# Weights split once and kept in DRAM: the split parts of a two-layer trunk's weights are made in the first segment and loaded by the later ones

## The chip, the core and the metric

The kernel runs on one core of a Trainium2 chip, in one launch. The metric is device time in microseconds (us), from runs of the whole program. Three runs of the kernel before gave 3135.08, 3143.48 and 3137.76 us, with a median of 3137.76 us.

## What is computed

Two layers of a decoder trunk act on one sequence of 2048 tokens, 1024 features wide, in float32:

```
for l in range(DEPTH):                       # DEPTH = 2
    shift, scale, gate = split(silu(c) @ ada_w[l] + ada_b[l], 3)
    h = rms_norm(x, norm_g[l]) * (1 + scale) + shift
    y = even_mixer(h) if l == 0 else odd_mixer(h)
    x = x + gate * y
```

- Layer 0 (even): `h @ w_in` (1024 x 3072) feeds a gated linear recurrence (4 heads, key and value 128 wide) and a causal pooling mixer (windows 2, 4, 8, 16). Each is multiplied by a SiLU gate, and both are joined and multiplied by `w_out` (1024 x 1024).
- Layer 1 (odd): `h @ w_in` (1024 x 4112) gives q, k, v and a SiLU gate for 16 heads of 64, and a forget value per head. Attention is causal, with normalised q and k and the summed log-forget as a bias; then `w_out` (1024 x 1024).

## The kernel before

The 2048 tokens are cut into four segments of 512 (SEG). A segment goes through both layers before the next one begins, so every weight is used four times, once per segment. Matrix products run at float32 accuracy out of products of "fp32r" operands: each operand is kept as two parts, a rounded one and the rest (value minus rounded value), and each product is made of three passes (PASSES: first with first, first with second, second with first).

**Weights.** Each weight matrix is cut into tiles of 1024 x 256: 12 for layer 0's input projection (kind "a"), 4 for its output (kind "b"), 16 for layer 1's input (kind "c"), 4 for its output (kind "d"), 36 in all. The list `wseq` holds the order in which tiles are used, over all segments: 144 uses and one special last entry "e" (the last two blocks of layer 1's output weights, times the gate). A tile in SBUF, `wt`, holds both parts, 128 partitions x 16 KB = 2 MB, in two buffers.

`prep_w(n)` (line 272) makes the n-th tile. It has four pieces. Each piece is loaded by SP's DMA queue into `raw` (256 KB, four buffers); ACT casts it into the first part (`S.copy`, line 289), and DVE or POOL, by turns, subtracts to make the second (`split_lo`, line 178). For the very first tile POOL does all four. The casts and subtractions have a lowered priority (`tc.cur_priority += 80`). `next_w` (line 294) hands out tile n and calls `prep_w(n + 1)`, so the work for the next tile starts when the tile before this one has given its buffer back. The raw pieces themselves can be in SBUF earlier.

**Layer 0 of a segment** (`layer0`): four heads of the recurrence, woven with projections (`fill`), then `out_proj0` (line 830): tile b0, then b1, then b2 and b3 side by side, both held at once.

**Layer 1 of a segment** (`layer1`, line 1226): the rows are normed and turned, tile c0 gives the first q and k, then 16 heads of attention, four by four. In segment s, a head goes over 4(s+1) blocks of 128 keys (`attend`, line 1114). Per block PE makes two score products (`pst`), ACT makes the exponential twice (`p` in float32, line 1152; `ph` rounded, line 1154), DVE subtracts to get `pl` (line 178), POOL adds `p` to a running sum `la` (line 1162), and PE multiplies `ph` and `pl` with the values (`pov`), two blocks later (LAG = 2). Beside it `max_pass` (line 1083) makes the next head's maxima: PE makes `pmx`, DVE reduces it (line 1094). Keys and values of earlier segments come back from DRAM in chunks of four blocks: `K1o` (two buffers), `Vo` (two), and `K2o` (three buffers, shared by `attend` and `max_pass`). These loads run on SP's queue, as the weights do. The small rows `mr` (the maxima), `q4d` and `cfd` go over ACT's DMA queue. The next projections (tiles c1 to c15, then the next segment's a0 to a3, or in the last segment the d tiles) are woven in as `fill`.

The order of each engine's instructions is made by a scheduler that takes priorities and its own timing of the instructions; it is fixed before the run.

Of the kernel before, what the change touches and what calls it, by code (L numbers as in the profile page):

```python
# [8 lines left out]
F32 = mybir.dt.float32  # L9
F32R = mybir.dt.float32r  # L10
# [5 lines left out]
PSUM = bass.MemoryType.PSUM  # L16
DRAM = bass.MemoryType.DRAM

P = 128
T = 2048  # L20
D = 1024
ND = D // P          # blocks of the model's width
SEG = 512            # tokens that go through both layers together
NSEG = T // SEG
NTB = SEG // P       # token blocks of a segment
NH = 16              # heads of the attention
HD = 64
# [5 lines left out]
def trunk(ctx, tc, x, cvec, norm_g, ada_c, ada_w, ada_b, ada_bg, lbp, w0, w0o, w1, w1f, w1o,  # L33
# [57 lines left out]
    # mq[q, k]: keys after the query, in the last block; mk[k, q]: the same with keys on the partitions  # L91
# [16 lines left out]
    # ones between zeros: the columns from HD on fill a pair's first head, those from 0 on its second  # L108
# [5 lines left out]
    # masks of the halving levels: right halves of each block, compact, for the chunks of a segment  # L114
# [12 lines left out]
    # 1 / min(t + 1, w) for the first positions  # L127
# [28 lines left out]
    def rsqrt_mean(out_t, ss, n, name):  # L156
        """out = 1 / sqrt(ss / n + eps) on a small tile"""
# [12 lines left out]
    def silu_from(out_t, src, t):  # L170
        """out = src * sigmoid(src); src may lie in PSUM, t is scratch"""
        S.activation(t, src, AF.Exp, scale=-1.0)
        S.activation(t, t, AF.Ln, bias=1.0)
        S.activation(t, t, AF.Exp, scale=-1.0)
        V.tensor_tensor(out_t, src, t, op=ALU.mult)
# [5 lines left out]
    class Steps:  # L181
        """a queue of generators, taken a step at a time"""
# [27 lines left out]
    def weave(main, nm, fill, keep=0):  # L210
        """the main stream's steps with the fill's spread evenly among them, but for the last ones to keep"""
# [12 lines left out]
    def both(*l):  # L224
        """generators by turns, a step of each; a number bounds how many steps the one before it takes"""
# [39 lines left out]
    # the last two blocks of the last projection's four tiles, times the gate  # L265
# [3 lines left out]
    wready = {}  # L269
    wpos = [0]  # L270

    def prep_w(n):
        if n >= len(wseq) or n in wready:
            return
        late = wseq[n][0] == "e"
        src = None if late else wsrc[wseq[n][0]][wseq[n][1]]
        wt = wp.tile([P, 2, ND, 256], F32R, name="wt", tag="wt")
        parts = range(3 if late else 4)
        if not late and n >= len(wseq) - 5:
            parts = range((NEARLY[wseq[n][1]] + 1) // 2)  # L280
        for h in parts:
# [9 lines left out]
            tc.cur_priority -= 80  # L291
        wready[n] = wt
# [12 lines left out]
    def proj_T2(pts, wt, act):  # L305
        """two tiles of 128 features, the second half of the contraction for the first token blocks first"""
# [14 lines left out]
    def proj_T(pt, wt, fo, act):  # L321
        """pt[feature, token] = the weights' 128 columns from fo on; two steps"""
# [8 lines left out]
    def proj_N(pt, wt, act, tb, ds=tuple(range(ND)), first=True, last=True):  # L331
        """pt[token of block tb, 256 columns], all of the contraction or some blocks of it"""
# [14 lines left out]
    def mod_cols(l, b, pm, which, n):  # L347
        """n columns of the shift (which = 0) or the scale (1) from their sums"""
# [8 lines left out]
    # which engine sums a block of the shift's and scale's products over d: PE, Vector, GpSimd  # L357
    WHO = ("GV", "PV", "GV", "PV", "GV", "VV", "VV", "VV")

    def ada_first(half, slots, between):  # L360
        """shift and scale of half of layer 0's features"""
# [51 lines left out]
    def ada_rest(scratch):  # L413
        """layer 0's gate, layer 1's shift and scale: products on the vector engine, sums on PE"""
# [31 lines left out]
    def norm_rows(xr, xt, stat=None):  # L446
        """the rows over their root mean square"""
# [934 lines left out]
```

## Time and profile before

| | |
|---|---|
| median of three runs | 3137.76 us (3135.08 to 3143.48) |
| span of the profiled execution (the one time the profile gives for it) | 3139.8 us |
| PE (TensorE) busy | 2830.8 us, 90% |
| DVE (VectorE) busy | 2505.1 us, 80% |
| ACT (ScalarE) busy | 1780.4 us, 57% |
| POOL (GpSimd) busy | 1226.5 us, 39% |
| mean granted TensorE clock | 0.967 |
| moved by DMA | 337.99 MB, mean 108 GB/s |

Busy times are shares of the whole span; the profile can also be asked for stretches of it. A row of the groups by line names the line of the kernel, the engine, the operation, the tile written and the tiles read, the shape and how often it ran; then come the total time, the mean of one in ns, and the engine's idle time just before these instructions with what ended it.

### The profile page before, as it was taken

The page shows a single profiled execution, that of the slowest core. Times are in us where ns is not written, and L with a number is a line of the kernel's source. Part 1 is how long each engine was busy: PE and PEld are TensorE (multiplying, and loading weights), DVE is VectorE, ACT ScalarE, POOL GpSimd, SP SyncE. Part 2 cuts the span into 40 slices and gives each one's busy share as a digit, 9 for nine tenths or more (in the row PEclk, how much of TensorE's full clock was granted, in tenths as well). Part 3 has the DMA queues.
Part 4 walks back from the last instruction along what each step waited for, and adds up shares of the span by engine and source line. Part 5 has one row for each costly group of instructions (what it writes and reads, how often), then busy time and mean ns, then how long its engine had stood idle before and what let it go on. Part 6 is the DMA issues. An engine that isn't in the chain of part 4 may idle for free. (4 is left out here: it accounts for less than half of the span.)

```text
span 3139.8 us, 49278 instructions
## 1 busy us (share of the span) xinstructions
PE 2830.8 (90%) x17020; PEld 2393.2 (76%) x17020; DVE 2505.1 (80%) x4518; ACT 1780.4 (57%) x3679; POOL 1226.5 (39%) x944
## 2 busy tenths in 40 slices
PE   5999899999998888899998888889999988888888
PEld 4788788888787777789897767777988866666666
DVE  8776697875868787875768888898666889898997
ACT  3454566753555566663555665666344566666653
POOL 3221232232123444343214555555311265656564
PEclk9999999999999999999999999999999999999999
DMA  6423453333333333334234333332423322222232
GB/s 241 161 78 108 124 150 100 113 105 101 96 115 99 94 104 98 109 91 122 76 124 121 99 112 105 114 118 90 132 75 106 100 88 90 91 92 90 89 121 66
DMA packets 198906, 337.99 MB, mean 108 GB/s; under 512 B 19768, under 2 KB 67000, under 8 KB 196096
## 3 DMA queue, kind: packets, MB, share of 16 engines
q1 hardware_dynamic: 195264, 320.93, 33.4%
q10 hardware_dynamic: 3392, 13.90, 1.3%
q8 instruction: 135, 2.21, 0.3%
q14 instruction: 115, 0.94, 0.1%
HBM read 285.33 MB, written 49.17 MB: 107 GB/s over the span
## 5 line engine op out<-in xcount | busy, mean ns | idle before, releaser
L178 POOL TENSOR_TENSOR wt<-raw,wt 128x512 fp32r<-128x512 f32 x287 | 431.0, 1509 | 1133.8 <-ACT wt L289 1034.8
L1162 POOL TENSOR_TENSOR la<-la,p 128x512 f32<-128x512 f32 (+3 forms) x528 | 670.5, 1270 | 516.5 <-ACT p L1152 451.2
L178 DVE TENSOR_TENSOR pl<-p,ph 128x512 fp32r<-128x512 f32 (+3 forms) x624 | 572.5, 921 | 49.4 <-ACT ph L1154 45.9
L1152 ACT ACTIVATE p<-pst 128x512 f32<-128x512 f32 (+3 forms) x624 | 333.8, 535 | 232.6 <-PE pst L39 173.3
L39 PE MATMUL pqk<-wt,h 128*128 128x256 f32 x3072 | 449.0, 288 | 5.6 <-DVE Vc L178 1.8
L39 PEld LDWEIGHTS pqk<-wt,h 128*128 128x128 f32 x3072 | 421.3, 195 | 24.1 <-issue 3.0
L39 PE MATMUL pgt<-h,wt 128*128 128x512 f32 x1536 | 422.5, 410 | 0.2
L289 ACT CAST wt<-raw 128x512 fp32r<-128x512 f32 x578 | 338.5, 626 | 81.6 <-PE py L39 37.5
L39 PE MATMUL pv<-wt,h 128*128 128x256 f32 x2304 | 352.8, 298 | 7.7 <-DVE h L178 4.8
L1154 ACT ACTIVATE ph<-pst 128x512 fp32r<-128x512 f32 (+3 forms) x640 | 342.7, 535 | 29.8 <-DVE pl L178 24.2
L39 PEld LDWEIGHTS pv<-wt,h 128*128 128x128 f32 x2304 | 326.2, 202 | 25.9 <-DVE h L178 7.7
L39 PEld LDWEIGHTS pgt<-h,wt 128*128 128x128 f32 x1536 | 294.2, 196 | 63.5 <-issue 2.7
L178 DVE TENSOR_TENSOR wt<-raw,wt 128x512 fp32r<-128x512 f32 x291 | 273.3, 942 | 54.9 <-ACT wt L289 53.8
L1094 DVE TENSOR_REDUCE mxs<-pmx 128x1 f32<-128x512 f32 x384 | 251.5, 682 | 23.5 <-PE pmx L39 22.8
L39 PE MATMUL pov<-pl,Vo 128*64 128x512 f32 x384 | 166.0, 432 | 109.5 <-DVE pl L178 104.3
L39 PE MATMUL py<-wt,o 128*128 128x256 f32 x1536 | 204.6, 289 | 0.0
L39 PE MATMUL py<-wt,mix 128*128 128x256 f32 x1536 | 199.0, 288 | 2.3 <-DVE yt L838 1.4
L39 PEld LDWEIGHTS py<-wt,o 128*128 128x128 f32 x1536 | 195.9, 195 | 4.1 <-issue 1.7
L39 PEld LDWEIGHTS py<-wt,mix 128*128 128x128 f32 x1536 | 187.9, 191 | 11.3 <-issue 6.5
L39 PEld LDWEIGHTS pov<-pl,Vo 128*64 128x64 f32 x384 | 53.1, 138 | 178.3 <-DVE pl L178 172.8
L39 PE MATMUL pov<-ph,Vo 128*128 128x512 f32 x384 | 163.5, 426 | 0.0
L39 PE MATMUL pst<-Q,K2o 68*128 68x512 f32 x384 | 150.7, 411 | 14.1 <-DMA K2o<-k2d 11.2
(378 smaller groups left out, 5329.8 us busy)
## 6 DMA issues: line engine op xcount, KB each, us to landing
raw<-in_w_dram SPq DMA_DIRECT2D x448, 256.0 KB
K2o<-k2d SPq DMA_DIRECT2D x192, 136.0 KB
K1o<-k1d SPq DMA_DIRECT2D x96, 256.0 KB
Vo<-vd SPq DMA_DIRECT2D x96, 256.0 KB
raw<-in_w1o_dram SPq DMA_DIRECT2D x66, 256.0 KB
raw<-in_w0o_dram SPq DMA_DIRECT2D x64, 256.0 KB
ada<-in_ada_w_dram ACTq DMA_DIRECT2D x12, 1024.0 KB
k1d<-K SPq DMA_DIRECT2D x48, 256.0 KB
```

The lines of the kernel that those rows point to most:

```text
L39: return nc.tensor.matmul(*a, **k)
L178: (eng or V).tensor_tensor(out_t, full, f(hi), op=ALU.subtract)
L289: S.copy(wt[:, 0, sl, :], raw)
L1094: V.tensor_reduce(mxs[:, i, c:c + 1], pm[:, 0:n], axis=AX.X, op=ALU.max)
L1152: S.activation(p[:, q0:], st[:, q0:], AF.Exp)
L1154: S.activation(ph[:, q0:], st[:, q0:], AF.Exp)
L1162: G.tensor_tensor(la[:, q0:], la[:, q0:], p[:, q0:], op=ALU.add)
```

## The change

In the first segment everything stays, and each finished tile, both parts, is also stored to DRAM (`wd`), by one DMA of 2 MB issued from ACT. When a tile of `wseq` comes up again, the later segment doesn't load, cast and subtract: it loads both parts from `wd` into `wt`, by two DMAs of 1 MB issued from SP. In the last segment the d tiles load only the blocks that are used there (NEARLY). Entry "e" is made as before. All else in the diff is comments taken out.

```
+    wd = {k: dr.tile([n, P, 2, ND, 256], F32, name="wd" + k) for k, n in (("a", 12), ("b", 4), ("c", 16), ("d", 4))}
...
+    wsplit = set()
     wpos = [0]
 
     def prep_w(n):
         if n >= len(wseq) or n in wready:
             return
         late = wseq[n][0] == "e"
+        if not late and wseq[n] in wsplit:
+            kind, i = wseq[n]
+            wt = wp.tile([P, 2, ND, 256], F32R, name="wt", tag="wt")
+            nd = NEARLY[i] if n >= len(wseq) - 5 else ND
+            for b in range(2):
+                nc.sync.dma_start(f(wt[:, b, 0:nd, :]), wd[kind][i, :, b, 0:nd, :])
+            wready[n] = wt
+            return
         src = None if late else wsrc[wseq[n][0]][wseq[n][1]]
         wt = wp.tile([P, 2, ND, 256], F32R, name="wt", tag="wt")
         parts = range(3 if late else 4)
-        if not late and n >= len(wseq) - 5:
-            parts = range((NEARLY[wseq[n][1]] + 1) // 2)
         for h in parts:
...
             split_lo(wt[:, 1, sl, :], raw, wt[:, 0, sl, :], G if (h % 2 or n == 0) and n < len(wseq) - 2 else V)
             tc.cur_priority -= 80
+        if not late:
+            wsplit.add(wseq[n])
+            nc.scalar.dma_start(wd[wseq[n][0]][wseq[n][1]], f(wt))
         wready[n] = wt
```

How the instructions stand on three queues, before and after. In the lines of the changed kernel, numbers above 180 are shifted by up to 12.

SP's queue in the last segment's attention. `K1o`, `K2o` and `Vo` are chunks of earlier keys and values; before:

```order
L1137 DMA K1o<-k1d 128x512
L1080 DMA K2o<-k2d 68x512
L1140 DMA Vo<-vd 128x512
L284 DMA raw<-in_w_dram 128x512 x3
L1137 DMA K1o<-k1d 128x512
L1080 DMA K2o<-k2d 68x512
L284 DMA raw<-in_w_dram 128x512
L1140 DMA Vo<-vd 128x512
L1080 DMA K2o<-k2d 68x512 x2
L1137 DMA K1o<-k1d 128x512
```

and in the changed kernel:

```order
L1092 DMA K2o<-k2d 68x512
L284 DMA wt<-wdc 128x2048 x2
L1152 DMA Vo<-vd 128x512
L1149 DMA K1o<-k1d 128x512
L1092 DMA K2o<-k2d 68x512
L1152 DMA Vo<-vd 128x512
L1092 DMA K2o<-k2d 68x512 x2
L1149 DMA K1o<-k1d 128x512
L1092 DMA K2o<-k2d 68x512 x2
L1152 DMA Vo<-vd 128x512
```

Four raw pieces of 256 KB, spread among the key and value loads, are replaced by one pair of 1 MB loads; this pair and the eleven that follow, up to the d tiles, all stand right ahead of a `Vo`.

ACT's queue in the first segment's attention, between the store of one head's maxima (`mr`) and what follows. `p` and `la` are the exponentials in float32, `u` a head pair's outcome; before:

```order
L1112 DMA Q_3609<-mr 2x4x128
L1065 ACTIVATE Q_3760<-pqkT,c_qkg 64x512
L1066 ACTIVATE K_3762<-pqkT,c_qkg 64x512
L1069 CAST Q_3761<-Q_3760 64x512
L1070 CAST K_3763<-K_3762 64x512
L289 CAST wt<-raw 128x512
L1152 ACTIVATE la<-pst 128x512
L1154 ACTIVATE ph<-pst 128x512
L289 CAST wt<-raw 128x512
L1192 ACTIVATE u<-pL 128x512
L1152 ACTIVATE p<-pst 128x384
```

and in the changed kernel:

```order
L1124 DMA Q_3634<-mr 2x4x128
L1077 ACTIVATE Q_3785<-pqkT,c_qkg 64x512
L1078 ACTIVATE K_3787<-pqkT,c_qkg 64x512
L1081 CAST Q_3786<-Q_3785 64x512
L1082 CAST K_3788<-K_3787 64x512
L1164 ACTIVATE la<-pst 128x512
L1166 ACTIVATE ph<-pst 128x512
L298 CAST wt<-raw 128x512
L1164 ACTIVATE p<-pst 128x384
L1204 ACTIVATE u<-pL 128x512
L303 DMA wdc<-wt 128x4096
L1205 ACTIVATE u<-u 128x512
```

The store of the finished tile (line 303) stands in the stream three instructions after the tile's last cast; it waits there for DVE's and POOL's subtractions, with the next exponentials behind it.

PE's order in the second segment's `out_proj0`, from tile b2 to tile b3 and on to the first tile of layer 1 (the number behind `wt` tells tiles apart, the one behind `py` the sums); before, wt_9037 is b1, wt_9193 b2, wt_9330 b3:

```order
L39 MATMUL py_9347<-wt_9193,mix_7893 128x256 x5
L39 MATMUL py_9269<-wt_9037,mix_7893 128x256 x24
L39 MATMUL py_9347<-wt_9193,mix_7893 128x256 x19
L39 MATMUL py_9414<-wt_9193,mix_7893 128x256 x9
L39 MATMUL py_9347<-wt_9330,mix_7893 128x256 x24
```

and in the changed kernel, wt_8895 is b1, wt_9037 b2, wt_9160 b3:

```order
L39 MATMUL py_9163<-wt_9037,mix_7863 128x256 x5
L39 MATMUL py_9099<-wt_8895,mix_7863 128x256 x24
L39 MATMUL py_9163<-wt_9037,mix_7863 128x256 x19
L39 MATMUL py_9230<-wt_9037,mix_7863 128x256 x23
L39 MATMUL py_9163<-wt_9160,mix_7863 128x256 x2
```

Between the last product with b1, which frees the buffer for b3, and the first with b3 stood 28 products; now there are 42.

## Rows read from the trace of the kernel before

**Rows 1.** The page's first part: span; busy time, share and instructions of engines.
```profile
span 3139.8 us, 49278 instructions
...
PE 2830.8 (90%) x17020; PEld 2393.2 (76%) x17020; DVE 2505.1 (80%) x4518; ACT 1780.4 (57%) x3679; POOL 1226.5 (39%) x944
```

**Rows 2.** Busy time by stretches: stretch and length, then each engine's busy us (instructions).
```profile
core 0: us, PE busy (x) PEld busy (x) DVE busy (x) ACT busy (x) POOL busy (x), PEclk, DMA share, GB/s
0.00:750.00 750.00, 674.33 (x4345) 595.21 (x4346) 567.79 (x1195) 402.20 (x848) 209.29 (x189) 0.97 0.42 131
...
350.00:700.00 350.00, 325.99 (x2119) 286.52 (x2120) 268.46 (x572) 223.20 (x473) 103.97 (x91) 0.97 0.40 118
...
950.00:1420.00 470.00, 415.89 (x2443) 350.52 (x2444) 384.78 (x689) 288.94 (x601) 195.75 (x155) 0.94 0.34 103
1420.00:1660.00 240.00, 233.00 (x1568) 208.90 (x1568) 161.37 (x320) 112.25 (x240) 56.96 (x38) 0.99 0.35 106
1660.00:2200.00 540.00, 476.96 (x2591) 380.94 (x2590) 473.44 (x780) 348.52 (x711) 282.82 (x211) 0.97 0.35 107
2200.00:2460.00 260.00, 252.95 (x1726) 228.50 (x1725) 179.24 (x354) 121.44 (x257) 61.39 (x44) 0.99 0.35 103
2460.00:3118.00 658.00, 567.69 (x2997) 443.72 (x2996) 589.42 (x888) 399.83 (x794) 379.03 (x278) 0.96 0.29 91
```

**Rows 3.** The page's costliest groups: the weights' casts and subtractions, whole program.
```profile
L178 POOL TENSOR_TENSOR wt<-raw,wt 128x512 fp32r<-128x512 f32 x287 | 431.0, 1509 | 1133.8 <-ACT wt L289 1034.8
...
L289 ACT CAST wt<-raw 128x512 fp32r<-128x512 f32 x578 | 338.5, 626 | 81.6 <-PE py L39 37.5
...
L178 DVE TENSOR_TENSOR wt<-raw,wt 128x512 fp32r<-128x512 f32 x291 | 273.3, 942 | 54.9 <-ACT wt L289 53.8
```

**Rows 4.** Waits of PE, attention of second, third and last segment: us, times, longest.
```profile
PE pov L39 <- DVE pl L178: 31.1, 27, 3.7
...
PE pov L39 <- DVE pl L178: 33.7, 51, 2.2
...
PE pov L39 <- DVE pl L178: 63.0, 95, 2.9
PE pst L39 <- DMA K2o<-k2d: 7.1, 11, 1.3
```

**Rows 5.** Groups by line, DVE, last segment's layer 1 (2460 to 3118 us).
```profile
L178 DVE TENSOR_TENSOR pl<-p,ph 128x512 fp32r<-128x512 f32 x255 | 253.8, 1000 | 15.9 <-ACT ph L1154 14.9 <-ACT r_qk L163 0.3
...
L178 DVE TENSOR_TENSOR ll<-la,lh 128x512 fp32r<-128x512 f32 x15 | 10.3, 684 | 0.2
```

**Rows 6.** Busy time by stretches, of instructions that read `raw` alone.
```profile
core 0: us, DVE busy (x) ACT busy (x) POOL busy (x), PEclk, DMA share, GB/s
950.00:1420.00 470.00, 35.44 (x40) 47.64 (x80) 59.61 (x40) 0.94 0.34 103
1660.00:2200.00 540.00, 37.46 (x36) 43.61 (x72) 52.15 (x37) 0.97 0.35 107
2460.00:3118.00 658.00, 50.42 (x46) 47.37 (x78) 52.01 (x35) 0.96 0.29 91
```

**Rows 7.** Busy time by stretches, the start: the fastest 8 us of the DMA engines.
```profile
12.00:20.00 8.00, 3.84 (x19) 3.85 (x19) 6.38 (x12) 1.13 (x6) 6.13 (x5) 1.00 1.01 423
```

**Rows 8.** Timeline of SP, then ACT: the first loads, and the first that waits.
```profile
2.20 1.85 SPq L716 DMA_DIRECT2D xt<-in_x_dram  x4
...
5.96 1.06 ACT L451 ACTIVATE junk<-xt 128x1024 bf16<-128x1024 f32 x1 [2.81 <-DMA xt<-in_x_dram]
```

**Rows 9.** Timeline of PE, end of second segment's layer 0: output products, then first q, k.
```profile
894.26 16.85 PE L39 MATMUL py<-wt,mix 128*128 128x256 f32 x135 [0.36 <-DVE yt L838]
...
915.78 0.95 PE L39 MATMUL pqk<-wt,h 128*128 128x256 f32 x6
```

## The prediction

> **What bounds the kernel now.** I read the busy times first. PE is busy for 2830.8 of 3139.8 us and DVE for 2505.1 [rows 1], so neither alone explains the span. An average over unlike stages hides which of them waits, so the second view is the busy time by stretches [rows 2]. There the kernel falls apart into two kinds. In layer 0 of the third and last segment (1420 to 1660, 2200 to 2460) PE is busy for 233.0 of 240 and 253.0 of 260 us, 97%, while DVE stands at 67 to 69%. Nothing but shorter PE work helps there. In layer 1 of the second, third and last segment (950 to 1420, 1660 to 2200, 2460 to 3118) PE is busy for 88%, 88% and 86%, and DVE rises with the length of the attention: 82%, 88%, 90%. PE's idle time in these three is 54 + 63 + 90 = 207 us, most of what it has. The third view says for what: the waits of PE [rows 4]. The product with the values waits for DVE's `pl` for 31.1, 33.7 and 63.0 us; the next in the last segment is a load of keys, 7.1 us. So in 1668 of 3140 us DVE is what PE waits for.
>
> The fourth view is the groups by line [rows 3, 5]. The weights' subtractions take 273 us of DVE and 431 of POOL, and the casts 339 of ACT. In the last segment DVE's `pl` takes 1000 ns on the mean, and `ll`, the same subtraction on the same shape but made when POOL's sum is already done, takes 684 ns. So POOL's work beside it costs DVE time too.
>
> **What is removed.** There are 144 uses of 36 tiles; 108 uses are now loads. Of 578 casts 36 x 4 + 3 = 147 are left, so 431 go; of DVE's 291 subtractions 73 are left, of POOL's 287, 74. At their means [rows 3] that is 431 x 0.626 = 270 us of ACT, 218 x 0.942 = 205 us of DVE, 213 x 1.509 = 321 us of POOL. Only what lies in the three attention stretches can shorten the kernel. There the instructions that read `raw` take 35.4, 37.5 and 50.4 us of DVE and 59.6, 52.2 and 52.0 of POOL [rows 6]; in the last, three subtractions and three products for "e" remain, 6 x 1.1 = 6.6 us. To this I add what POOL's share costs `pl`: in the last segment 255 x (1.000 - 0.684) = 81 us over 379 us of POOL, 0.21 us for each, so 11 to 13 us a stretch. DVE loses 48, 48 and 55 us.
>
> What that is worth has two ends. If DVE kept its share of each stretch, the stretch would shrink in proportion: 48/384.8 x 470 = 59, 48/473.4 x 540 = 55, 55/589.4 x 658 = 61 us, together 175. If PE's waits for `pl` come from the length of a chain and not from DVE's load, the gain is nothing. Between them stands a stretch with less DVE load, the first segment's layer 1 (350 to 700): DVE 77%, PE 326.0 of 350, 93.1%. At that share PE's busy times give 415.9/0.931 = 447, 512 and 610 us, so 23 + 28 + 48 = 99 us. DVE would then stand at 75%, 83% and 88%. I take **99**: in the last stretch it is somewhat much, in the second somewhat little.
>
> The lower ACT load and the freed POOL I cost at nothing: ACT's stretches are at 61 to 65%, and POOL idled 1134 us ahead of its weight pieces [rows 2, 3]. In layer 0 the gain is nothing, PE covers it.
>
> **What is added: loads.** A tile is now 2.097 MB and not 1.049. The DMA engines' fastest stretch moved 423 GB/s at full share [rows 7], so a tile takes 4.96 us at least. The first row load, 0.524 MB or 1.24 us at that rate, was issued at 2.20 and used at 5.96 us [rows 8], so 2.5 us go to what is fixed, and a tile takes about 7.5 us from issue to use (an estimate). The Trainium skill, page "DMA: Bandwidth & Descriptors", section "Specifications", gives about 358 GB/s as a core's limit from HBM, which would make a tile 5.9 + 2.5 us; the 423 GB/s of the trace are above it, so I don't use it.
>
> The load starts when the tile before has given its buffer back, and is wanted when the next tile is used up. A tile of 96 products takes 96 x 16.85/135 = 12.0 us [rows 9], so in plain streams 7.5 us are covered. Not covered is the change from layer 0 to layer 1. The load of b3 starts when b1 ends, and 42 products, 5.2 us, stand between: 2.2 us of waiting. c0 takes b2's buffer, free about 24 products ahead of layer 1's turns; PE began c0's products at 915.78 us, about 5 us after b2's last, so it would wait 2 to 3 us more; I take 2. In three segments that is 3 x 4 = **12 us**; at worst both loads lie bare, 3 x 2 x 7.5 = 45; at least nothing.
>
> The third place is the keys and values. In the last segment a block takes 658/256 = 2.6 us, and 16 of the 20 new tiles are issued in the midst of such loads. I take it that a load behind a pair of 1 MB on the same queue lands up to 4.96 us later (no row shows a pair). `K2o` has three buffers for two readers, and PE waited for it 11 times already, 7.1 us in all [rows 4]: these loads come just in time, so a delay passes on. At least it costs nothing (the old pieces stood in the same queue), at most 4.96 us for each of 60 tiles, 298 us. I take 20 us in the last segment, 10 in the third, 3 in the second: **33**.
>
> **What is added: stores.** 36 stores of 2.097 MB, 75 MB in the first 750 us, where 131 GB/s flow at a DMA share of 0.42 [rows 2]: room enough. But the store is issued by ACT, which stands still until POOL's last piece is done, a POOL piece of 1.5 us after the last cast [rows 3]: 36 x 1.5 = 54 us. ACT is busy for 402 of 750 us [rows 2], and PE for 90%, so I put a third of it on the path, 18 us. `mr`, 16 times, can land behind a store in ACT's queue, up to 4.96 us late, 79 us; the stores cover about 36 x 5 of 750 us, so a quarter of the heads could meet one, at half that: 8 us. Sum **26**, between nothing and 130.
>
> **Sum.** -99 + 12 + 33 + 26 = -28 us on the profiled execution's 3139.8, so 3111.8. Its span is 2.0 us above the median of the runs, so the forecast is **3110 us**.
>
> **Rivals.**
> 1. *DVE's relief is half spent.* In the stretches after the first, DVE's load stays above the 77% of the comparison, so PE's 93% isn't reached: all of 23, three quarters of 28, half of 48 is 68 us, and 3139.8 - 68 + 71 = 3143, no change. For it speaks the last stretch's 88%. Against it, that PE waits for `pl` in all three. Chance 0.16.
> 2. *Keys behind weights: slower.* In the attention of the three later segments the pair of 1 MB holds `K2o` and `Vo` back, and PE waits for DMA where it waited for DVE. If a third of the 60 tiles cost 4.96 us each, that is 99 us in place of 33: 3139.8 - 99 + 12 + 99 + 26 = 3178. It decides from 61 us on, where the gain is gone: 12 tiles at the full price. For it speak the order (the pair right ahead of `Vo`) and the 11 waits; against it a chunk of four blocks, 10 us, between loads of one kind. Chance 0.25, with whatever else goes wrong in the first segment.
> 3. *DVE and POOL share one resource, and it is the bound.* `pl` and `ll` show POOL stretching DVE. If a subtraction and a POOL operation never ran together, the last stretch would hold 379 us of POOL + 255 x 0.684 + 43 x 0.684 = 583 of 658 us. Without the weights 79 us go there, 77 and 87 in the two others: 243, so 3139.8 - 243 + 71 = 2968. The Trainium skill, page "SBUF — State Buffer", section "Who interferes with whom", says that a DVE operation with two SBUF inputs and a GpSimd one that reads SBUF exclude each other for whole instructions. The trace agrees in kind; a full exclusion would add more than the 0.32 us that `pl` shows if its turn were at random. Against it as the bound: PE's own 86 to 88%. Chance 0.04.
>
> That the change doesn't do what it says can be left out: the order shows 108 pairs of loads in place of casts.
>
> **How the numbers follow.** The forecast has 0.55, with 3040 to 3128: its low end takes 150 us of gain and 50 of costs, its high end 80 and 71, to where a difference counts. About 0.3% (9 us) is what a measurement of this kernel can tell from no change. Faster by more: 0.55 + 0.04 = 0.59; within: 0.16; slower: 0.25. The range reaches from 3040 to 3170, which takes in rival 1 and over half of rival 2.
>
> **What would show it.** Right: DVE's busy time down by some 50 us in each attention stretch, PE's waits for `pl` clearly below 63 us in the last one, the stretch itself 40 to 50 us shorter, layer 0 as long as before; ACT waiting at the stores for 1 to 2 us each. Wrong: PE waiting for `K2o`, `K1o` or `Vo` for over 60 us in sum, or for `wt` in layer 0, or a first segment over 50 us longer.

## The result and the profile after

The changed kernel is slower: 3172.5 us median of four runs (3168.0 to 3181.8) against 3140.6 us, a ratio of 1.0106 (95% interval 1.0089 to 1.0122). The forecast was 3110 us, with a range from 3040 to 3170. The profiled execution spans 3171.8 us, 32.0 us more than that of before.

The page's first part, changed kernel:

```profile
span 3171.8 us, 47644 instructions
...
PE 2840.9 (90%) x17020; PEld 2398.5 (76%) x17020; DVE 2206.2 (70%) x4300; ACT 1566.8 (49%) x3248; POOL 889.8 (28%) x731
```

Beside [rows 1], DVE lost 299 us of work, POOL 337 and ACT 214, and the kernel became longer. Of DVE's 299 us the subtractions that are gone make 213 (291 took 273.3 us [rows 3], the 73 that are left take 60.3); the other 86 us are instructions that the change leaves as they were and that became shorter. PE has the same 17020 products. To see where the time went, stretches of the clock no longer do, since the two executions drift apart. I cut both at events that both have: the issue of a row of maxima (`mr`), 16 in each segment. The first and the sixteenth of them mark the heads of a segment's layer 1. Busy time by stretches cut there, kernel before; the rows are the first segment up to its first row of maxima, its heads, then by turns the stretch between (the last head, the output and the next segment's layer 0) and the heads of the next segment, without the last 56.5 us:

```profile
core 0: us, PE busy (x) PEld busy (x) DVE busy (x) ACT busy (x) POOL busy (x), PEclk, DMA share, GB/s
0.00:360.40 360.40, 309.71 (x1896) 270.58 (x1896) 274.11 (x588) 166.79 (x355) 90.28 (x88) 0.97 0.44 146
360.40:645.30 284.90, 262.59 (x1722) 229.56 (x1723) 225.27 (x488) 189.34 (x406) 83.32 (x75) 0.97 0.40 116
...
645.30:960.10 314.80, 305.37 (x2034) 273.99 (x2033) 215.04 (x417) 153.27 (x319) 76.18 (x54) 0.98 0.35 107
960.10:1362.30 402.20, 348.09 (x2016) 290.23 (x2015) 332.98 (x598) 251.09 (x527) 168.14 (x135) 0.93 0.33 99
1362.30:1680.40 318.10, 309.16 (x2055) 276.66 (x2053) 222.64 (x425) 157.41 (x326) 84.99 (x58) 0.99 0.35 106
1680.40:2166.30 485.90, 426.98 (x2316) 339.31 (x2315) 433.01 (x719) 315.02 (x646) 260.92 (x195) 0.96 0.36 109
2166.30:2494.70 328.40, 316.23 (x2080) 281.73 (x2080) 230.67 (x433) 162.21 (x335) 88.57 (x62) 0.98 0.34 101
2494.70:3083.30 588.60, 506.56 (x2640) 391.92 (x2639) 533.31 (x808) 364.18 (x726) 350.80 (x258) 0.97 0.31 96
```

The same of the changed kernel, without the last 54.5 us:

```profile
0.00:386.80 386.80, 314.73 (x1861) 273.21 (x1862) 268.23 (x587) 165.86 (x355) 82.85 (x88) 0.93 0.65 236
386.80:708.70 321.90, 278.35 (x1758) 240.16 (x1758) 215.01 (x484) 184.12 (x395) 73.08 (x69) 0.94 0.58 201
...
708.70:1016.40 307.70, 298.27 (x2007) 267.74 (x2006) 171.46 (x383) 119.15 (x250) 25.65 (x20) 0.99 0.52 188
1016.40:1425.30 408.90, 358.91 (x2044) 301.63 (x2043) 282.07 (x568) 223.50 (x467) 119.21 (x105) 0.91 0.42 140
1425.30:1740.00 314.70, 306.66 (x2032) 274.83 (x2031) 170.41 (x383) 114.84 (x242) 19.54 (x16) 0.98 0.48 174
1740.00:2226.80 486.80, 425.26 (x2339) 336.67 (x2338) 391.10 (x688) 284.87 (x586) 212.36 (x165) 0.97 0.44 143
2226.80:2548.00 321.20, 311.77 (x2066) 278.19 (x2065) 178.60 (x391) 119.03 (x250) 24.89 (x20) 0.99 0.47 172
2548.00:3117.30 569.30, 502.68 (x2650) 388.79 (x2648) 492.09 (x776) 333.85 (x663) 309.00 (x229) 0.98 0.38 127
```

Read the second column against the one above. The first segment, up to its last row of maxima, took 645.3 us and takes 708.7: **63 us lost**, 26 ahead of the heads and 37 in them. 21 us of the loss are PE's busy time, for as many products (3618 and 3619) at a lower granted clock (0.93 and 0.94 against 0.97); PE's waits there grew from 72.5 to 115.0 us. All that follows took 2494.5 and takes 2463.1: **31 us won**, of which 19 lie in the last segment's heads. The second segment's heads became 7 us longer, although DVE does 51 us less there.

What PE waits for in the later segments (from 709 us on) tells why. Waits of PE in us, times, longest; changed kernel:

```profile
PE pov L39 <- DVE pl L180: 69.1, 134, 2.8
PE pst L39 <- DMA Q<-mr: 65.0, 34, 3.4
PE py L39 <- DMA wt<-wdb: 11.2, 5, 3.7
PE pov L39 <- DMA K1o<-k1d: 10.5, 6, 1.8
PE pst L39 <- DMA K2o<-k2d: 10.3, 13, 2.6
PE pqkT L42 <- DVE qk L1030: 8.0, 12, 0.9
```

and before, from 646 us on:

```profile
PE pov L39 <- DVE pl L178: 128.3, 175, 3.7
PE pqkT L42 <- DVE qk L1018: 30.8, 18, 2.6
...
PE pst L39 <- DMA K2o<-k2d: 11.2, 17, 1.3
```

The wait for `pl` fell by 59 us, as hoped, and the one for `qk`, which DVE makes too, by 23. In their place PE waits 65.0 us for `Q<-mr`: the rows of maxima, 4 KB, that ACT's queue carries into `Q` at the end of each head. In the whole kernel before it waited 5.0 us for them. Nothing of the change touches these rows. One of them, in the second segment; timeline of the changed kernel (start us, us, engine, line, what; in brackets the idle time before and its releaser):

```profile
1089.48 0.81 SPq L284 DMA_DIRECT2D wt<-wdc  x2
...
1090.79 0.62 ACTq L1124 DMA_DIRECT2D Q<-mr  x1
...
1093.37 0.39 PE L39 MATMUL pst<-Q,K1o 128*128 128x512 f32 x1
...
1096.66 0.80 PE L39 MATMUL pst<-Q,K2o 68*128 68x512 f32 x1 [2.90 <-DMA Q<-mr]
```

The same moments as busy time of PE by stretches, with the granted clock, the share of the DMA engines and GB/s:

```profile
core 0: us, PE busy (x), PEclk, DMA share, GB/s
...
1093.00:1094.00 1.00, 0.76 (x6) 1.00 1.03 434
1094.00:1095.00 1.00, 0.00 (x0) 1.00 1.07 452
1095.00:1096.00 1.00, 0.00 (x0) 1.00 0.99 409
1096.00:1097.00 1.00, 0.34 (x1) 0.53 0.23 94
1097.00:1098.00 1.00, 1.00 (x3) 0.50 0.06 16
1098.00:1100.00 2.00, 2.00 (x9) 0.50 0.00 0
```

SP issues the pair of 1 MB, 1.3 us later ACT the row. The row stands in another queue, but the same engines carry both: they are full until 1096, and so long the row isn't there. PE then runs at a granted clock of 0.50, that is at 1.2 GHz, after 2.9 us of idling: the wait costs once as idle time and once more behind it.

The packets in the trace give the rows' time from the issue to the end of the last packet: 1.7 us on the mean in the second segment before, 4.4 us now, and 5.1 to 5.5 us for nine of its 16. At three of its heads no pair is issued in the 6 us before the row, and there it is 1.4 us. The meeting is no accident. A quad's four tiles are spread evenly over its four heads, so a tile is used up, its buffer given back and the next load started when a head ends; and then the maxima of the next head are sent. The Trainium skill, page "DMA: Bandwidth & Descriptors", section "Queues, rings and completion order", says that each DMA engine takes turns between the queues that have work for it, a packet at a time. The trace fits this in part. The eight packets of the row above come from 4.1 to 5.1 us after its issue, two every 0.33 us, about as long as one of the pair's packets of 8 KB takes (0.35 us on the mean), and the pair's last ends at 6.0 us. But the first of them comes after 4.1 us and, in the heads without a pair, after 1.3; turns alone don't give that, and no run here shows what does.

### The profile page after: what moved, and what is told of

It is laid out like the page before. It is cut to its first block, busy times and chain, and to the rows that moved or that the text cites. A ratio compares the mean times of both kernels' runs of the same rounds, so it can differ in the third digit from the quotient of the medians.

```text
span 3171.8 us, 47644 instructions
## 1 busy us (share of the span) xinstructions
PE 2840.9 (90%) x17020; PEld 2398.5 (76%) x17020; DVE 2206.2 (70%) x4300; ACT 1566.8 (49%) x3248; POOL 889.8 (28%) x731
## 4 chain that ended last, share of the span: by engine, by line
PE 58%; DVE 20%; DMA 12%; ACT 5%; issue 4%; POOL 0%; SPq 0%; ACTq 0%; DVEq 0%; POOLq 0%
PE py L39 9%; PE pqk L39 9%; PE pgt L39 8%; DVE pl L180 6%; DMA Q<-mr 6%; PE pst L39 5%; PE pov L39 4%; PE pv L39 4%; PE pmx L39 3%; PE pl L39 3%; PE pf L39 3%; PE pq L39 3%; PE pu L39 3%; DVE mxs L1106 2%; DMA K2o<-k2d 2%
## 5 line engine op out<-in xcount | busy, mean ns | idle before, releaser
L1174 POOL TENSOR_TENSOR la<-la,p 128x512 f32<-128x512 f32 (+3 forms) x528 | 656.5, 1243 | 673.7 <-ACT p L1164 599.6
L180 DVE TENSOR_TENSOR pl<-p,ph 128x512 fp32r<-128x512 f32 (+3 forms) x624 | 560.4, 902 | 125.2 <-ACT ph L1166 121.9
L39 PE MATMUL pqk<-wt,h 128*128 128x256 f32 x3072 | 437.5, 291 | 7.1 <-DVE Vc L180 3.5
L39 PE MATMUL pgt<-h,wt 128*128 128x512 f32 x1536 | 411.4, 403 | 0.0
L1166 ACT ACTIVATE ph<-pst 128x512 fp32r<-128x512 f32 (+3 forms) x640 | 342.1, 534 | 32.6 <-DVE pl L180 29.7
L1172 POOL TENSOR_TENSOR la<-p 128x512 f32<-128x512 f32 x48 | 62.8, 1308 | 1037.0 <-ACT p L1164 1000.5
L39 PE MATMUL pv<-wt,h 128*128 128x256 f32 x2304 | 344.9, 296 | 4.7 <-DVE h L180 2.5
L39 PE MATMUL pst<-Q,K2o 68*128 68x512 f32 x384 | 160.6, 438 | 77.2 <-DMA Q<-mr 65.0
L180 POOL TENSOR_TENSOR wt<-raw,wt 128x512 fp32r<-128x512 f32 x74 | 106.1, 1442 | 408.5 <-ACT wt L298 356.6
L39 PE MATMUL py<-wt,mix 128*128 128x256 f32 x1536 | 202.0, 291 | 13.7 <-DMA wt<-wdb 11.2
L39 PE MATMUL pst<-Q,K1o 128*128 128x512 f32 x384 | 161.8, 429 | 2.9 <-ACT ph L1166 2.0
L39 PE MATMUL pmx<-K2o,Q 68*128 68x512 f32 x384 | 152.5, 425 | 8.5 <-DVE K L1080 3.3
```

What stands on the lines that cost most here:

```text
L39: return nc.tensor.matmul(*a, **k)
L180: (eng or V).tensor_tensor(out_t, full, f(hi), op=ALU.subtract)
L1166: S.activation(ph[:, q0:], st[:, q0:], AF.Exp)
L1172: G.tensor_tensor(la, first, p, op=ALU.add)
L1174: G.tensor_tensor(la[:, q0:], la[:, q0:], p[:, q0:], op=ALU.add)
```

## Experiments: are the two parts what they seem?

**stores_only**, **reload_one_tile**. One keeps the stores and undoes the reloads, the other keeps the reloads and all but one store.

```
 stores_only:      -        if not late and wseq[n] in wsplit:
                   +        if False:
 reload_one_tile:  -            nc.scalar.dma_start(wd[wseq[n][0]][wseq[n][1]], f(wt))
                   +            if n == 0:
                   +                nc.scalar.dma_start(w1st, f(wt))
                   -  ... wd[kind][i, :, b, 0:nd, :])
                   +  ... w1st[:, b, 0:nd, :])
```

> The changed kernel without its reloads: all 36 tiles are stored in the first segment, and every later use is loaded raw, cast and subtracted as before the change. Theory (the stores lengthen the first segment by 63 us, whatever the later segments do): 3140 + 63 = 3203, between 3190 and 3215, the sixteenth store of maxima rows at about 709 us as in the changed kernel. Rival (the first segment is longer because its instructions stand in another order, and not because of the stores' traffic): the order differs here too, so it would be told apart only by what waits; if the time is 3140 to 3160 the loss comes from the reloads, which then reach back into the first segment.

> The changed kernel with one store in place of 36: only the first tile is stored, and every later use loads that same 2 MB tile (so the later segments multiply with the wrong weights; their instructions, loads and sizes are those of the changed kernel). Theory (first segment +63 from the stores, later segments -31): 3140 - 31 = 3109, between 3095 and 3120, with the waits of PE for the maxima rows (Q from mr) still near 65 us. Rival (the first segment's loss isn't the stores'): 3165 to 3175.

Measured: 3210.0 us, ratio 1.0236 (1.0213 to 1.0258), and 3102.6 us, 0.9893 (0.9872 to 0.9914). The sixteenth row of maxima goes out at 710.3 us with the stores and at 645.4 without. The two parts are separate and add up (71 less 36 is 35 us; both together cost 32): the stores cost 71 us, 65 of them in the first segment, and the reloads win 36, although the rows' waits are in them (58 us of PE's time).

**lead_two_steps**, **before_lead**. The woven projections run two steps, half a head, ahead, in the first three quads.

```
-            while fill.n > keep + (nf - keep) * (nm - i - 1) / nm and fill.step():
+            while fill.n > max(keep, keep + (nf - keep) * (nm - i - 1) / nm - lead) and fill.step():
...
-            weave(quad_attention(s, quad, fill), 16 * (s + 1), fill, keep=2 if more else 0)
+            weave(quad_attention(s, quad, fill), 16 * (s + 1), fill, keep=2 if more else 0, lead=2 if quad < 3 else 0)
```

> The changed kernel, with the projections that are woven into the first three quads of heads two steps ahead, so that a weight tile is used up, and the next one's load starts, in the middle of a head and not at its end, where the maxima rows are sent. Theory (the 4 KB rows of maxima, on ACT's queue, wait on the DMA engines behind the 2 MB that SP issued about 1 us before): the rows land after 1.4 us again and not after 4 to 5, PE's wait for them falls from 70 us to under 20, and the time to 3172 - 50 = 3122, between 3110 and 3135. Rival (PE would wait for pl or for keys anyway, so that the wait only changes its name): 3160 to 3180 with the waits for pl or for K2o, K1o and Vo longer by some 50 us.

> The kernel before, with the same two steps of lead: the control for the run above. Theory (there is no large load to move away from the maxima rows, whose waits are 5 us): 3130 to 3150. Rival (the lead is good in itself, for the projections come earlier): 3110 or less.

Measured: 3107.8 us, 0.9914 (0.9891 to 0.9936), and 3139.9 us, 1.000 (0.998 to 1.002). The lead alone does nothing; beside the reloads it is worth 65 us, 54 of them after the first segment. The other 11 lie in a segment without reloads; in the control this segment is 9 us shorter too (636.5 against 645.3) and the later ones together 8 us longer, so only the 54 are counted to the rows. What is left of the rows' wait in the later segments, and the second segment's heads:

```profile
PE pst L39 <- DMA Q<-mr: 18.0, 9, 2.6
```
```profile
1005.60:1366.90 361.30, 333.56 (x2044) 279.16 (x2043) 284.06 (x568) 223.23 (x467) 128.29 (x105) 1.00 0.47 159
```

408.9 us have become 361.3. The same 2044 products take 333.6 us of PE in place of 358.9, for the granted clock is 1.00 and not 0.91: of 48 us, 25 are the clock and 22 the idle time. The rows land after 1.4 us in 12 of 16 heads; in the four that begin a quad they still take 3.5 to 4.3. Of the 47 us that the wait for the rows lost, 19 came back as waits for `pl` (87.8 in place of 69.1); those for keys and values didn't grow (19 in place of 26). So a part of the wait did change its name, but the rival, with its 3160 to 3180 us, falls.

**reload_in_pieces**. The changed kernel without lead, each reload as eight loads of 256 KB.

```
-                nc.sync.dma_start(f(wt[:, b, 0:nd, :]), wd[kind][i, :, b, 0:nd, :])
+                for h in range((nd + 1) // 2):
+                    sl = slice(2 * h, min(nd, 2 * h + 2))
+                    nc.sync.dma_start(f(wt[:, b, sl, :]), wd[kind][i, :, b, sl, :])
```

> The changed kernel itself, no lead, with each reload cut from two loads of 1 MB into eight of 256 KB. Theory (a row waits for what has been issued ahead of it: SP needs about 0.4 us for each issue, so only two or three pieces stand ahead of a row sent 0.9 us after the first): the rows land after 2 to 3.5 us in place of 4.4 to 5.5 in the second segment, PE's waits for them fall from 70 us to 25 to 45, and the time to 3135 to 3155. Rival (the pieces pile up all the same, since 256 KB take 0.6 us and an issue 0.4): 3160 to 3175.

Measured: 3128.3 us (ten runs, 3122.9 to 3147.8), a ratio of 0.9976 (0.9955 to 0.9996). PE's wait for the rows falls from 70.3 to 42.8 us, and the time by 44, more than expected (3135 to 3155): the size of what is issued ahead of the row counts. In the second segment's 13 heads with a load the rows land after 3.1 to 3.8 us in place of 4.4 to 5.5, later than the 2 to 3.5 expected: the pieces do pile up, only less.

## Experiments: what makes the stores dear?

All of these have the two steps of lead, so they stand beside lead_two_steps: 3107.8 us, its sixteenth row at 697.9. In the changed kernel DVE waits for the loads of the layer gates' weights, which share ACT's queue with the stores; waits of DVE to 700 us, changed kernel:

```profile
DVE ada L412 <- DMA ada<-in_ada_w_dram: 17.6, 4, 9.1
...
DVE aacc L412 <- DMA aw<-in_ada_w_dram: 7.1, 1, 7.1
```

Before, it was 3.6 us in all. ACT stands for DVE's and POOL's splits for 14 us (15 in lead_two_steps).

**lead_store_sp**, **lead_store_pool**, **lead_store_later**. The store is issued from SP (`nc.sync`), from POOL (`nc.gpsimd`), or from ACT one tile later:

```
 later:  +        while unsaved:
         +            k, t = unsaved.pop()
         +            nc.scalar.dma_start(wd[k[0]][k[1]], f(t))
         ...
         -            nc.scalar.dma_start(wd[wseq[n][0]][wseq[n][1]], f(wt))
         +            unsaved.append((wseq[n], wt))
```

> The run with two steps of lead, with the 36 stores issued from SP in place of ACT. Its first segment still takes 698 us against 645 before. Theory A (what costs is ACT's queue: the loads of the layer gates' weights, 1 MB each, and the rows of maxima stand behind 2 MB stores there, and ACT itself stands still for the splits): DVE's waits for those loads fall from 24 to under 10 us, the first segment to 655 to 675 us, the time to 3065 to 3085. Theory B (it is the traffic on the shared DMA engines, by whichever queue it goes): the first segment stays at 690 to 705, the time at 3100 to 3115. Theory C (SP now stands at the store until DVE and POOL have split, with the raw pieces, keys and rows behind it): the first segment over 710 us, the time over 3120.

> The run with two steps of lead, with the 36 stores issued from POOL, which makes half of the pieces itself and is busy for 22% of the first segment. Theory A (ACT's queue is what costs): 3065 to 3085, as with SP. Theory B (traffic): 3100 to 3115. Theory C for this queue (POOL stands at the stores, its sums la and its pieces come late, or its queue costs more for each transfer): over 3120.

> The run with two steps of lead and the stores on ACT's queue, but each store is issued one tile later, when the next tile's preparation begins and the splits are long done, so ACT never stands still for them; the 2 MB stores still stand in the one queue with the gates' weights and the rows of maxima. Theory A1 (ACT's standing, 16 us of waits for the splits and what hangs on it, is the larger part of what SP's queue won back, 30 us): 3075 to 3092. Theory A2 (the order within ACT's queue is: loads and rows behind a store): 3098 to 3115, DVE's waits for the gates' weights still over 18 us.

Measured: from SP 3073.1 us, 0.9779 (0.9739 to 0.9819), sixteenth row at 668.5; from POOL 3108.1, 0.9895 (0.9872 to 0.9918), at 700.7; one tile later 3109.9, 0.9916 (0.9883 to 0.9948), at 694.6. One tile later ACT waits for the splits for 1.4 us only, and the time is the same; so ACT's standing still, on which my price of the stores rested, costs nothing that shows. Nor is it ACT's queue as such: from POOL it costs as much, in another place (there PE waits 35.3 us for the rows of maxima within the first segment's heads, from SP 16.5). From SP, the queue that carries the raw pieces too, the first segment is 23 us longer than before and not 53. DVE's waits for the gates' weights fall to 13.1 us there, not under 10 as theory A had it.

**lead_c_only**, **lead_c_only_sp**. Only the 16 tiles of kind c are stored and reloaded.

```
-        if not late:
+        if wseq[n][0] == "c":
             wsplit.add(wseq[n])
```

> The run with two steps of lead, with only layer 1's 16 input tiles (kind c) stored and reloaded; a, b and d are made raw each time, as before. Theory (the relief lies in layer 1's attention alone, layer 0 is covered by PE; the 20 other stores only cost): the first 386 us of the program take 358 to 362 again, PE's waits for wdb (11 us) are gone, and the time is 3070 to 3085. Rival (the a and d tiles made beside the attention of quad 3 and the b tiles matter as much as c): 3100 to 3120.

> Two steps of lead, only the c tiles stored and reloaded, and the stores from SP. Theory A: both savings add, first segment 650 us or less, 3050 to 3070. Theory B: as with ACT's queue, 3070 to 3085. Theory C: 3085 or more.

Measured: 3104.6 us, 0.9878 (0.9851 to 0.9905), and from SP 3076.9, 0.9799 (0.9768 to 0.9829), no better than with all 36 tiles. The first row of maxima goes out at 355.2 us again and not at 386.2, so 31 us of the loss belong to the tiles of layer 0. But the first segment's heads give 4 of them back and the later segments 22: 9 in the stretches with layer 0 and 14 in the heads, beside whose last four the tiles of kinds a and d are made. The time is the rival's (3100 to 3120). That layer 0 has no use for the relief, as my theory had it, is at odds with the 9 us; what follows says more.

**best_early_load**, **best_store_pieces**. On lead_store_sp: the tile after next is loaded as soon as the values' projection has emitted its last product; then also each tile stored in four pieces.

```
+                if t2 + j == 2:
+                    prep_w(wpos[0] + 1)
                 yield
 pieces:  +            if not late:
          +                nc.sync.dma_start(wd[wseq[n][0]][wseq[n][1], :, :, sl, :], f(wt[:, :, sl, :]))
```

> The run with two steps of lead and the stores from SP, and the load after next of a tile is issued when the values' projection has emitted its last products, so that the first tile of a quad's projections no longer starts its load at the quad's first head. In the four heads that begin a quad the rows of maxima still landed after 3 to 4 us in every later segment. Theory (same mechanism, four places a segment): those fall to 1.4 us, PE's waits for the rows from 30 to under 18 us, the time from 3073 to 3055 to 3068. Rival (the wait moves to keys or to pl): 3070 to 3085.

> The best run (two steps of lead, stores from SP, early load; 3060 us) with each tile stored in four pieces of 512 KB, each issued by SP when its quarter is split. Theory (what hurts is how long one 2 MB store holds the DMA engines, with rows and pieces behind it): the first segment from 661 to 646 to 653 us, the time 3045 to 3055. Rival 1 (the volume costs): unchanged, 3055 to 3066. Rival 2 (SP now stands four times a tile for a split): the first segment over 668, the time over 3068.

Measured: 3060.5 us, 0.9750 (0.9728 to 0.9771), and 3059.6, 0.9753 (0.9725 to 0.9781). The first lies in the range expected, but not for the reason: PE's wait for the rows is 34.1 us, no less than before this step (29.7), and of the 23 us between the two profiled spans (the medians differ by 13) 17 lie in the last segment's heads (569.4 to 552.2). What made these shorter I have not found. The pieces change nothing: from SP, at least, it isn't how long one store holds the engines. Nor can it be the volume alone, since from SP the same volume costs less than half. What makes SP's queue the cheaper one stays open.

## Experiments: where does the relief come from?

**dve_half_kept**, **pool_half_kept**, **pool_memset**. On lead_store_sp, each reloaded tile has two subtractions of 128x512 again, into a scratch tile, by DVE or by POOL; or POOL reads one column and writes zeros three times.

```
+            for h in (0, 2):
+                extra = wp.tile([P, 2, 256], F32, name="extra", tag="raw", bufs=4)
+                V.tensor_tensor(extra, f(wt[:, 0, 2 * h:2 * h + 2, :]), f(wt[:, 1, 2 * h:2 * h + 2, :]), op=ALU.subtract)
 pool_half_kept:  G.tensor_tensor in its place
 pool_memset:     three times G.memset(extra, 0.0) in its place
```

> The run with two steps of lead and the stores from SP; in the later segments each reloaded tile also makes DVE do two subtractions of 128x512 into a scratch tile, at the lowered priority, as many as DVE had before the change (ACT's casts and POOL's pieces stay away; the results aren't used). Theory (the later segments' 85 us come from DVE's 205 us that are gone): 60 to 85 us are lost again, 3133 to 3158. Rival (they come from ACT's casts, or from POOL's pieces, which stretch pl): under 3100.

> As the run before, but the two subtractions of each reloaded tile are done by POOL and none by DVE. Theory (POOL's pieces cost only what they stretch pl by, 0.21 us for each us of POOL, some 11 to 13 us a stretch, and only part of that shows): 3078 to 3100. Rival (DVE and POOL share one resource that is the bound, so 321 us of POOL cost as much as DVE's own): over 3125.

> As the run that kept POOL's half (3154), but in place of each subtraction of 128x512 POOL reads one column of the new tile (so that it waits for its load as before) and then fills the scratch tile three times with zeros, about 1.5 us, without reading. Theory (POOL's two reads from SBUF stretch DVE's work: with the same instructions DVE was busy for 24 us more in the last attention): 3075 to 3100. Rival (POOL's time itself delays its sums la, and these hold the buffers of p): 3140 to 3165.

Measured, beside 3073.1 us: DVE's half costs 38 (3111.5; ratio to before 0.9902, 0.9876 to 0.9929), POOL's half 81 (3154.0; 1.0045, 1.0021 to 1.0069), the zeros 28 (3101.0; 0.9878, 0.9863 to 0.9893). Both of the first two theories were wrong, and the second one's rival (over 3125) came: the engine that nobody waits for was the dearer one. The zeros came out at the edge of their theory (3075 to 3100). The busy lines of the pages of lead_store_sp, pool_half_kept and pool_memset:

```profile
PE 2809.0 (91%) x17020; PEld 2376.9 (77%) x17020; DVE 2209.4 (72%) x4300; ACT 1566.3 (51%) x3248; POOL 918.2 (30%) x731
```
```profile
PE 2835.6 (90%) x17020; PEld 2398.5 (76%) x17020; DVE 2321.3 (74%) x4300; ACT 1570.0 (50%) x3248; POOL 1234.2 (39%) x947
```
```profile
PE 2812.7 (91%) x17020; PEld 2385.7 (77%) x17020; DVE 2242.2 (72%) x4300; ACT 1567.8 (51%) x3248; POOL 1277.8 (41%) x1595
```

Look at DVE: the same 4300 instructions take 111.9 us more when POOL makes 216 subtractions beside them, 0.52 us for each, and 32.8 us more when POOL only writes, though it is busy for longer. It is mostly POOL's reading that DVE pays for. It doesn't pay in all its instructions. One with two inputs in SBUF (`Dt` and `kT`) and one whose first input, the sum `py`, lies in PSUM; groups by line of the same three runs, in the same order:

```profile
L600 DVE TENSOR_TENSOR Dt<-Dt,kT 128x256 f32<-128x256 f32 x112 | 49.8, 445 | 0.0
L605 DVE TENSOR_TENSOR Dt<-Dt,kT 128x256 f32<-128x256 f32 x112 | 58.4, 521 | 0.0
L607 DVE TENSOR_TENSOR Dt<-Dt,kT 128x256 f32<-128x256 f32 x112 | 50.2, 448 | 0.0
```
```profile
L850 DVE TENSOR_TENSOR yt<-py,gate 128x256 f32<-128x256 f32 x64 | 26.1, 422 | 85.9 <-PE py L39 85.8
L855 DVE TENSOR_TENSOR yt<-py,gate 128x256 f32<-128x256 f32 x64 | 26.1, 421 | 84.2 <-PE py L39 84.2
L857 DVE TENSOR_TENSOR yt<-py,gate 128x256 f32<-128x256 f32 x64 | 26.1, 422 | 87.5 <-PE py L39 87.5
```

The Trainium skill, page "SBUF — State Buffer", section "Who interferes with whom", says that a DVE instruction with two inputs in SBUF shuts out a GpSimd one that reads SBUF, and the other way round, but not one that only writes. The trace agrees on the larger part: added up by operation, 80 of 115 us lie in DVE's TENSOR_TENSOR, and beside the zeros these are 7 us shorter. What the zeros add lies mostly in TENSOR_SCALAR (34.5 us); for that no run here shows a cause.

**before_dve_only**, **before_dve_all**, **best_dve_only**. If that is so, the kernel before needs no stored tiles: its subtractions only have to leave POOL. In the first of the three this is done from the second segment on, in the second everywhere but for the first tile; the third does the latter on best_early_load.

```
-            split_lo(wt[:, 1, sl, :], raw, wt[:, 0, sl, :], G if (h % 2 or n == 0) and n < len(wseq) - 2 else V)
+            split_lo(wt[:, 1, sl, :], raw, wt[:, 0, sl, :], G if (h % 2 or n == 0) and n < 36 else V)
 all:  +  ... G if n == 0 else V)
```

> The kernel before, with all subtractions of the weights in the later three segments on DVE and none on POOL (the first segment as it was). Theory (a POOL piece costs the path more than a DVE piece: 81 us for 216 against 38): 3139 - 81 + 38 = 3096, between 3085 and 3120. Rival (DVE, at 82 to 90% in the three attentions, becomes the bound): 3160 or more.

> The kernel before, with all subtractions of the weights on DVE but for the first tile's, also in the first segment: no stores, no reloads. Theory (as above, 3056 - 14): 3042, between 3030 and 3052. Then the stored tiles are worth nothing beyond it, if best_dve_only doesn't lie under it by more than 9 us. Rival (DVE has no room left in the first 360 us, at 76% beside the modulation): 3054 or more.

> The run with two steps of lead, stores from SP and early load (3060 us), with the first segment's subtractions on DVE alone, but for the first tile's. Theory (a POOL piece costs the path about 0.4 us more than nothing, 81 us for 216, and a DVE piece 0.18): 70 pieces times 0.2 us, 3060 - 14 = 3046, between 3035 and 3055. Rival (the first segment is held by traffic and latency, not by DVE): 3056 to 3066.

Measured: 3056.1 us, 0.9728 (0.9714 to 0.9743); 3032.3 us, **0.9664** (0.9642 to 0.9685); 3044.2 us, 0.9696 (0.9674 to 0.9718). The first is well under the 3085 to 3120 expected, the other two lie in their ranges. One word in the kernel before gives more than the stored tiles at their best, and with it they are worth nothing: best_dve_only is 12 us behind. The page of before_dve_only, beside [rows 1]:

```profile
PE 2793.7 (91%) x17020; PEld 2363.0 (77%) x17020; DVE 2489.8 (81%) x4731; ACT 1777.2 (58%) x3679; POOL 927.6 (30%) x731
```

DVE does 213 instructions more and is busy for 15 us less. Groups by line in the second segment's layer 0 (645.3 to 960.1 us), kernel before:

```profile
L178 DVE TENSOR_TENSOR wt<-raw,wt 128x512 fp32r<-128x512 f32 x42 | 39.9, 955 | 13.9 <-ACT wt L289 13.8
L582 DVE TENSOR_TENSOR Dt<-cT 128x256 f32<-128x256 f32 x28 | 18.4, 659 | 0.0
```

and the same stretch of before_dve_only (638 to 939.9 us):

```profile
L178 DVE TENSOR_TENSOR wt<-raw,wt 128x512 fp32r<-128x512 f32 x81 | 54.4, 703 | 12.4 <-ACT wt L289 12.3
...
L582 DVE TENSOR_TENSOR Dt<-cT 128x256 f32<-128x256 f32 x28 | 12.4, 442 | 0.0
```

81 subtractions cost 54.4 us where 42 cost 39.9, and the recurrence's `Dt`, which has nothing to do with the weights, takes 442 ns and not 659; the three like it change by 19 ns at most. This stretch became 13 us shorter, in a layer that I had put at nothing. With the two later ones of its kind it is 36 of the 77 us that the later segments gain.

## Why the prediction was wrong

- **The bound.** That DVE's load in layer 1 was what PE waited for held: the wait for `pl` fell from 128.3 to 69.1 us in the later segments, and to 87.8 where the rows of maxima are out of the way.
- **The relief, 99 us.** Nearly right in size. With the rows of maxima out of the way (lead_two_steps) the later segments are 85 us shorter, after the waits for `wdb` and the keys are paid. But its make-up was wrong twice. I priced POOL's share by what it stretches `pl`, 11 to 13 us a stretch; the mean of `pl` hardly moved in the long form (128x512: 1076 ns before, 1062 in the changed kernel, 1089 in lead_store_sp); that POOL's own sums, which run beside it in any case, keep it there is likely, but not shown. The stretch lay in the other instructions of DVE, in layer 0 too, where "the gain is nothing, PE covers it". Kept alone, POOL's half costs 81 us, DVE's 38.
- **The change of layer, 12 us.** Right in sum, and partly by luck: PE waits 11.2 us for `wdb`, 3.4 to 3.7 us at a time in each segment where 2.2 were expected, and 1.3 us in all for tiles of kind c where it should have been 6.
- **Keys and values behind weights, 33 us.** Too much. PE waits 10.3 us for `K2o` and 10.5 for `K1o`, where it was 11.2 for `K2o`; with the shorter waits it is 26 us for keys and values against 12, so 14 were added.
- **The step that failed first** is the one on added loads. It asked only what stands behind the pair *on the same queue*. The smallest transfer of all, on ACT's queue and at the end of a head's chain, was counted behind stores in the first segment, and not behind the loads in the other three. There it cost 54 us (2463.1 against 2409.2 after the first segment). 20 of these are PE's busy time (2247.9 against 2227.7 us for the same products), which the granted clock makes longer; the sum had no term for that.
- **The step that failed second** is the price of the stores: 26 us, measured 63 to 65. Two thirds of it stood for ACT waiting for the splits, which costs nothing (lead_store_later). What PE's record shows of the 63 is 21 us of longer products at the lower clock, and 18 us of waits, where it was 1, for sums that DVE makes of the gates' weights (`ada`, line 412). How the stores bring about the rest, and why they cost less than half from SP, stays open. (A slip in the sum itself: a quarter of 16 heads at half of 4.96 us is 10 us and not 8; nothing hangs on it.) "Room enough" was read from a mean share of 0.42; it is 0.65 now up to the heads. A first segment over 50 us longer was among my own signs of being wrong, and it came.
- **Rival 2** gave 3178 and the sign, but by keys; the delay hit the row of maxima. **Rival 3** had half of its mechanism right: POOL's reading does stretch DVE's work, by 0.52 us for each piece, but spread over DVE's other instructions and not over `pl`, the only place where I looked. That it is the bound, the other half, no run shows; its 2968 us are under every time measured here. I gave the whole 0.04, since I only asked whether it was the bound.

The whole in one line, on the spans: 3139.8 - 85 (relief, net of new waits for tiles and keys) + 54 (rows of maxima) + 63 (stores) = 3171.8.

## What to carry to other kernels

Ask of every large transfer which small one is on its way at the same moment, on any queue, and whether the program's own rhythm makes them meet; here a shift by half a head was worth 54 to 65 us. Before taking work away from an engine by way of memory, move it: the 213 subtractions that POOL did "for nothing" cost DVE as much as doing them itself. And price a wait of PE with the stretch at the lower clock behind it.

## What was not expected of the hardware

- A row of 4 KB took up to 5.5 us, in place of 1.4, because 2 MB had been issued on another engine's queue 1.3 us before.
- 216 subtractions by POOL made 4300 unchanged instructions of DVE 111.9 us longer; the same POOL time with writes alone 32.8 us.
- After 2.9 us without a product the granted clock was 0.50 for the next 3 us at least. Over the second segment's heads it came to 0.91 against 1.00, and 358.9 against 333.6 us for the same 2044 products.
